# Issuing the loads and stores of the down-projection's weight sums on GpSimd's queue

## The chip, the cores and the metric

The kernel runs on one core of a Trainium2 chip. The metric is the device time of one execution in microseconds. Before the change three runs took 1840.31, 1840.57 and 1843.14 us; the median is 1840.57 us.

The core has five engines with instruction queues of their own: PE (matrix multiply), DVE (vector), ACT (scalar), POOL (GpSimd) and SP (sync). Each works through its queue in order and waits on semaphores for the others. A transfer between DRAM and the on-chip memory is issued by an instruction on one of these queues and then moved by 16 DMA engines, which all queues share. In this kernel nearly all transfers are issued by SP. GpSimd issues a few hundred in the middle of the program, for the attention.

## The reference

The reference is one layer of a diffusion backbone over 1024 latent tokens and 256 context tokens with 1024 channels: modulated norm, one input projection, neighbourhood attention beside a long convolution, an output projection, and then the feed-forward part with which this case is concerned:

```python
h2 = _rmsnorm(x, norm2_g) * (1.0 + sc2) + sh2
u = _dwconv3(h2 @ w_up, ffn_conv_w, ffn_conv_b)
gate, up = jnp.split(u, 2, axis=-1)
x = x + g2 * ((jax.nn.silu(gate) * up) @ w_down)
```

`w_up` is 1024 x 5632 and `w_down` is 2816 x 1024, all in float32. `_dwconv3` is a convolution of width 3 along the tokens.

## The kernel before, in words

A float32 product is made of three matmuls of a split pair (a high part and the rest): `mm3`, lines 116 to 118. `split`, lines 121 and 122, makes the pair: ACT copies the high part (L121), and DVE subtracts it to get the rest (L122).

Both products of the feed-forward part are done with Strassen's scheme in Winograd's form: a product of 2 x 2 blocks takes seven block products in place of eight, at the price of sums of blocks before and after. For the up-projection the sums of the weight blocks are made on DVE as the tiles arrive (L1519 to L1525, tiles `S`). For the down-projection four sums of the blocks of `w_down` are needed, and they are made ahead of time, while the up-projection runs, and kept in a DRAM tensor `tdr`.

The up-projection is a loop over 22 blocks `f` of 128 gate channels and 128 up channels. A step of the loop, in the order of the code, does this:

- load one tile `wt` of the down-projection's weights (L1595): 128 partitions x 2 x 2 x 256 floats, 512 KB, in two transfers of 256 KB, one for each half `r`;
- `up`: load two tiles `wr` of `w_up` (512 KB each, L1503), make the sums, split them into `ws`, and run seven block products on PE, each 24 matmuls, 168 in all. ACT copies some results out (L1547), and DVE adds the others to them into the rows of `rows` (L1552);
- make the four sums in place in `wt` (L1597 to L1600 on DVE, 128 x 256 each), and store the tile to `tdr` (L1602), again in two transfers of 256 KB;
- `conv`: the convolution of the gate rows and of the up rows into `cv` (L1579 on ACT, L1580 and L1581 on DVE), the SiLU (L1604), the product (L1606);
- store the product to `gdr` (L1607, L1608), and, in the first half of the loop, a difference of two halves of it (L1610, L1611) to `sdr` (L1612).

The tile `wt` has one buffer (`bufs=1`). So the next load waits until both stores of the tile before have landed, and the first sum waits until the next load's first half has landed. The tiles `wr` have three buffers.

The order of the instructions on each engine is not that of the code. A scheduler places them by a timeline of its own, so the 22 tiles `wt` do not go one to a step: they are placed as early as the timeline lets them, two to a step, and all 22 are through in the first half of the loop. A change of a queue therefore also moves instructions on the other engines.

The down-projection follows the loop. It reads `gdr`, `sdr` and `tdr` back, and its seven block products use `w_down` itself or the sums. In the changed lines `Q` is SP's queue and `G` is GpSimd's; `wdn` is `w_down` seen by blocks, and `cs` picks a 256 column part of the block.

Of the kernel before, what the change touches and what calls it, by code (L numbers as in the profile page):

```python
# [77 lines left out]
def build(tc, I, O, dbg=None, upto=99):  # L78
    nc = tc.nc
    V, A, G, T, Q = nc.vector, nc.scalar, nc.gpsimd, nc.tensor, nc.sync  # L80
    dbg = dbg or {}
    top = ExitStack()
    with top:
        _build(nc, tc, top, V, A, G, T, Q, I, O, dbg, upto)


def _build(nc, tc, top, V, A, G, T, Q, I, O, dbg, upto):
# [194 lines left out]
    def ft(shape, tag, dt=F32, bufs=1):  # L282
        return fp.tile(shape, dt, tag=tag, name=tag, bufs=bufs)
# [216 lines left out]
    with ies:  # L500
# [3 lines left out]
        for gi, (s, col, tl) in enumerate(groups):  # L504
# [22 lines left out]
            cs = slice(col, col + P * len(tl))  # L527
# [74 lines left out]
    def wsplit(pl, src, scale):  # L602

        i = turn_("w")
        w = pl.tile([P, KC, P], F32, tag=f"wr{i}", name="wr", bufs=1)
        wloads.append(Q.dma_start(out=w, in_=src).ins)
        wh = pl.tile([P, KC, P], F32R, tag=f"wh{i}", name="wh", bufs=1)
        wl = pl.tile([P, KC, P], F32R, tag=f"wl{i}", name="wl", bufs=1)
        if scale == 1.0:
            split(w, wh, wl)  # L610
        else:
            A.activation(wh, w, AF.Copy, scale=scale)
            V.scalar_tensor_tensor(wl, w, scale, wh.bitcast(F32), op0=ALU.mult, op1=ALU.subtract)
        return wh, wl
# [122 lines left out]
    for j in range(4):  # L737
        for which in range(3):
            hy_chunk(which, j)
            if j + which == 0:  # L740

                t = ft([P, 512], "tm", bufs=2)
# [738 lines left out]
    tdr = dr.tile([NI, P, 2, 2, 512], F32, name="tdr")  # L1481
    wdn = I["w_down"][0].rearrange("(r k p) (b c) -> k p r b c", r=2, k=NI, b=2)
    NC = LC + 1 + LL

    def rows():

        t = acp.tile([P, 5 * D], F32, tag="acc", name="rows", bufs=1)
        w = NC + 2
        return [t[:, i * w:(i + 1) * w] for i in range(3)], [t[:, 3 * w + i * NS[1]:3 * w + (i + 1) * NS[1]] for i in range(2)]
# [40 lines left out]
    def up(f, rg, ru):  # L1530

        ws = blocks(f)

        def prod(outs, p, start, stop):
            w = next(ws)
            for s in range(2):
                t = TT[s][p]
                for k in range(4):
                    ks = slice(k * P, (k + 1) * P)
                    mm3(outs[s][:, :NS[s]], w[:, 0, ks], w[:, 1, ks], t[:, 0, k], t[:, 1, k], start and k == 0,  # L1540
                        stop and k == 3)

        def cp(src):
            t = [fpl.tile([P, NS[0]], F32, tag="pc", name="pc", bufs=2), pcb[ring["pc"] % 2]]
            ring["pc"] += 1
            for s in range(2):
                A.copy(t[s], src[s][:, :NS[s]])  # L1547
            return t

        def add(r, cols, x, y):  # L1550
            for s in range(2):
                V.tensor_add(cells(r, cols)[s], j3(x[s]), j3(y[s][:, :NS[s]]))  # L1552

        def two(tag):
            return [bk(tag) for _ in range(2)]

        a = two("a")
        prod(a, 0, True, True)
        p1 = cp(a)
        b = two("b")  # L1560
        prod(b, 1, True, True)
        add(rg, 0, p1, b)
        c = two("c")
        prod(c, 4, True, True)
        p5 = cp(c)
        prod(a, 5, False, True)
        u1 = cp(a)
        prod(c, 2, False, True)
        add(rg, 1, u1, c)
        prod(a, 6, False, True)  # L1570
        add(ru, 1, p5, a)
        d = two("b")
        prod(d, 3, True, True)
        u2 = cp(a)
        add(ru, 0, u2, d)

    def conv(r, ch):
        cv = fpl.tile([P, NC], F32, tag="cv", name="cv", bufs=2)
        A.activation(cv, r[:, 1:NC + 1], AF.Identity, scale=ffw(1, ch), bias=ffb(ch))  # L1579
        V.scalar_tensor_tensor(cv, r[:, 0:NC], ffw(0, ch), cv, op0=ALU.mult, op1=ALU.add)  # L1580
        V.scalar_tensor_tensor(cv, r[:, 2:NC + 2], ffw(2, ch), cv, op0=ALU.mult, op1=ALU.add)  # L1581
        return cv

    for f in range(NFF):
        if f == 0:
            raw, pcb = rows()
            for r in raw:
                for c in (0, LC + 1, NC + 1):
                    G.memset(r[:, c:c + 1], 0.0)
        rg, ru = raw[2 * f % 3], raw[(2 * f + 1) % 3]  # L1590

        i, cs = f // 2, slice(f % 2 * 256, f % 2 * 256 + 256)
        t = fpl.tile([P, 2, 2, 256], F32, tag="wt", name="wt", bufs=1)
        for r in range(2):
            Q.dma_start(out=t[:, r], in_=wdn[i, :, r, :, cs])  # L1595
        up(f, rg, ru)
        V.tensor_sub(t[:, 0, 0], t[:, 0, 1], t[:, 0, 0])  # L1597
        V.tensor_sub(t[:, 0, 1], t[:, 1, 1], t[:, 0, 1])
        V.tensor_sub(t[:, 1, 1], t[:, 1, 1], t[:, 0, 0])
        V.tensor_sub(t[:, 1, 0], t[:, 1, 1], t[:, 1, 0])  # L1600
        for r in range(2):
            Q.dma_start(out=tdr[i, :, r, :, cs], in_=t[:, r])  # L1602
        ga = conv(rg, f)
        A.activation(ga, ga, AF.Silu)  # L1604
        u_ = conv(ru, NFF + f)
        V.tensor_mul(ga, ga, u_)  # L1606
        Q.dma_start(out=gdr[f, :, 0:LC], in_=ga[:, 0:LC])  # L1607
        Q.dma_start(out=gdr[f, :, LC:], in_=ga[:, LC + 1:NC])  # L1608
        if f < NI:
            V.tensor_sub(u_[:, 0:LC], ga[:, 0:LC], ga[:, NR + 1:NR + 1 + LC])  # L1610
            V.tensor_sub(u_[:, LC:NR], ga[:, LC + 1:NR + 1], ga[:, NR + 1 + LC:])  # L1611
            Q.dma_start(out=sdr[f], in_=u_[:, 0:NR])  # L1612
# [20 lines left out]
    def gsplit(src, lasting=None):  # L1633

        if lasting is None:
            hl = dp.tile([P, 2, NR], F32R, tag="gs", name="gs", bufs=3)
            hl = hl[:, 0], hl[:, 1]
        else:
            hl = [dp2.tile([P, NR], F32R, tag=f"X{2 * lasting + x}", name="gx", bufs=1) for x in range(2)]
        split(src, *hl, V)  # L1640
        return hl
# [142 lines left out]
    cs = [(gsplit(Z[i], i - NI + NT), wsplit("4", i, T4)) for i in range(NI - NT, NI)]  # L1784
    for j in range(5):
        for i, (g, w) in enumerate(cs):
            dmm(ps[j], g, w, j, False, i == NT - 1)
        t = dp2.tile([P, 512], F32, tag="fx", name="t", bufs=3)
# [44 lines left out]
```

## Time and profile before

| | |
|---|---|
| median of 3 runs | 1840.57 us |
| the profiled execution, its own time | 1844.13 us |
| its span, first to last instruction | 1841.7 us |
| PE busy | 1719.3 us, 93% of the span |
| DVE busy | 1369.6 us, 74% |
| ACT busy | 893.9 us, 49% |
| GpSimd busy | 396.2 us, 22%; nothing between 1007 and 1700 us |
| DMA queue that SP feeds | 230.75 MB |
| DMA queue that GpSimd feeds | 16.46 MB |
| up-projection's loop | about 995 to 1560 us |
| loads and stores of `wt` issued | 1005.0 to 1278.9 us |

The profile is of one execution, 3.6 us longer than the median of the runs. In the views below the times are microseconds from the start of the span. A row of a timeline has the start, the duration, the engine, the line, the operation with its tiles, and in brackets how long the engine sat idle before it and what released it. Durations of DVE instructions overlap a little with the next one's start (some 0.09 us), so the distance from one start to the next is what counts in a sum. "SPq" and "POOLq" mean the queue of that engine, where an instruction that only issues a transfer is not counted as busy.

### The profile page before, as it was taken

The numbers are of one execution on the slowest core, as the hardware profiler recorded it, in microseconds if no ns is written. First come the engines' busy times: TensorE is split into PE (matmuls) and PEld (weight loads), VectorE is DVE, ScalarE is ACT, GpSimd is POOL, SyncE is SP. The second block draws the span as 40 slices with busy tenths as digits, with TensorE's granted clock in tenths as the row PEclk, the third lists the DMA queues.
The fourth block names the chain that finished last, engine by engine and source line by source line (L and its number), as shares of the span: only waits on it lengthen the run. The fifth ranks groups of instructions, "written<-read, shape, count | busy, mean of one in ns | idle before, by whom it ended". The sixth has DMA issues, their size and how long they took to land.

```text
span 1841.7 us, 27321 instructions
## 1 busy us (share of the span) xinstructions
PE 1719.3 (93%) x9979; PEld 1448.2 (79%) x9979; DVE 1369.6 (74%) x2168; ACT 893.9 (49%) x1852; POOL 396.2 (22%) x487
## 2 busy tenths in 40 slices
PE   5899999999995898898996999999999999999997
PEld 2688788788784455565885999999999999888786
DVE  4668957852778798974568788888777787556797
ACT  4755545532434666665546444444444444443452
POOL 2366655673126432501000000000000000000001
PEclk7999999999996799998998999999999999999999
DMA  7424354356446332516221554454222213934653
GB/s 272 143 75 143 113 169 123 119 146 206 144 140 189 95 113 58 147 47 205 87 97 63 159 173 145 157 163 158 82 68 71 67 57 108 342 113 143 207 185 131
DMA packets 202439, 249.76 MB, mean 136 GB/s; under 512 B 21923, under 2 KB 147988, under 8 KB 202050
## 3 DMA queue, kind: packets, MB, share of 16 engines
q1 hardware_dynamic: 190360, 230.75, 38.9%
q0 software_dynamic: 10240, 16.46, 3.7%
q8 instruction: 78, 1.28, 0.3%
q10 hardware_dynamic: 1705, 0.82, 0.2%
q14 instruction: 56, 0.45, 0.1%
HBM read 176.75 MB, written 71.20 MB: 135 GB/s over the span
## 4 chain that ended last, share of the span: by engine, by line
PE 39%; DVE 14%; DMA 7%; ACT 4%; issue 3%; POOL 2%; SPq 0%; DVEq 0%; POOLq 0%; ACTq 0%
PE psd L118 6%; PE psd L116 6%; PE psd L117 6%; DMA wt<-in_w_down_dram 3%; PE psa L116 2%; PE psa L117 2%; PE psa L118 2%; PE psc L117 2%; PE psc L118 2%; PE psc L116 2%; PE psb L117 2%; PE psb L118 2%; PE psb L116 2%; DMA tdr<-wt 2%; DVE cv L1581 1%
## 5 line engine op out<-in xcount | busy, mean ns | idle before, releaser
L116 PE MATMUL psp<-hh,wh 128*128 128x512 f32 (+1 forms) x552 | 200.7, 364 | 1.9 <-ACT wh L121 1.9
L118 PE MATMUL psp<-hh,wl 128*128 128x512 f32 (+1 forms) x552 | 199.1, 361 | 0.0
L117 PE MATMUL psp<-hl,wh 128*128 128x512 f32 (+1 forms) x552 | 199.1, 361 | 0.0
L1748 POOL TENSOR_TENSOR rs<-rs,mhalf 128x1 f32<-128x1 f32 x10 | 7.7, 775 | 821.6 <-DVE rs L1747 821.6
L116 PE MATMUL psa<-T,ws 128*128 128x256 f32 (+1 forms) x528 | 166.0, 314 | 8.7 <-ACT rows L1547 7.6
L117 PE MATMUL psa<-T,ws 128*128 128x256 f32 (+1 forms) x528 | 165.1, 313 | 0.0
L118 PE MATMUL psa<-T,ws 128*128 128x256 f32 (+1 forms) x528 | 164.6, 312 | 0.0
L116 PE MATMUL psd<-wd,gs 128*128 128x512 f32 x360 | 141.1, 393 | 3.1 <-ACT gs L121 3.1
L117 PE MATMUL psd<-wd,gs 128*128 128x512 f32 x360 | 141.2, 392 | 0.0
L118 PE MATMUL psd<-wd,gs 128*128 128x512 f32 x360 | 125.5, 392 | 1.8 <-DVE gs L122 1.8
L116 PEld LDWEIGHTS psp<-hh,wh 128*128 128x128 f32 x552 | 105.0, 190 | 23.2 <-issue 7.4
L118 PEld LDWEIGHTS psp<-hh,wl 128*128 128x128 f32 x552 | 104.6, 189 | 15.2 <-issue 1.2
L117 PEld LDWEIGHTS psp<-hl,wh 128*128 128x128 f32 x552 | 105.0, 190 | 14.0 <-issue 0.4
L116 PE MATMUL psc<-T,ws 128*128 128x384 f32 (+1 forms) x352 | 110.0, 313 | 6.1 <-ACT ws L121 6.1
L117 PE MATMUL psc<-T,ws 128*128 128x384 f32 (+1 forms) x352 | 110.0, 313 | 0.0
L967 POOL DMA_DIRECT2D tb<-rpw x192 | 100.3, 530 | 45.3 <-DVE m L1089 27.8
L116 PEld LDWEIGHTS psa<-T,ws 128*128 128x128 f32 x528 | 101.3, 192 | 10.7 <-ACT rows L1547 9.0
L118 PE MATMUL psc<-T,ws 128*128 128x384 f32 (+1 forms) x352 | 109.6, 312 | 0.0
L117 PE MATMUL psb<-T,ws 128*128 128x384 f32 (+1 forms) x352 | 109.4, 311 | 0.0
L118 PE MATMUL psb<-T,ws 128*128 128x384 f32 (+1 forms) x352 | 109.4, 311 | 0.0
L116 PE MATMUL psb<-T,ws 128*128 128x384 f32 (+1 forms) x352 | 109.2, 310 | 0.0
L117 PEld LDWEIGHTS psa<-T,ws 128*128 128x128 f32 x528 | 101.2, 192 | 0.0
(404 smaller groups left out, 4771.2 us busy)
## 6 DMA issues: line engine op xcount, KB each, us to landing
wada<-in_w_ada_dram SPq DMA_DIRECT2D x48, 512.0 KB
wr<-in_w_up_dram SPq DMA_DIRECT2D x44, 512.0 KB
gr<-gdr SPq DMA_DIRECT2D x44, 320.0 KB
wr<-in_w_in_dram SPq DMA_DIRECT2D x23, 512.0 KB
wt<-in_w_down_dram SPq DMA_DIRECT2D x44, 256.0 KB
tdr<-wt SPq DMA_DIRECT2D x44, 256.0 KB
gdr<-cv SPq DMA_DIRECT2D x22, 512.0 KB
wr<-tdr SPq DMA_DIRECT2D x20, 512.0 KB
```

The lines of the kernel that those rows point to most:

```text
L116: T.matmul(out, ah, bh, start=start, stop=False, skip_group_check=True)
L117: T.matmul(out, ah, bl, start=False, stop=False, skip_group_check=True)
L118: T.matmul(out, al, bh, start=False, stop=stop, skip_group_check=True)
L967: blast[0] = G.dma_start(out=tv[:, :, a * 8:a * 8 + 64], in_=rpw[var, :, 2 * p_:2 * p_ + 2, :, d * 8:d * 8 + 64].rearrange("q h u x -> q ( ...
L1581: V.scalar_tensor_tensor(cv, r[:, 2:NC + 2], ffw(2, ch), cv, op0=ALU.mult, op1=ALU.add)
L1748: G.tensor_tensor(rs, rs, mhalf, op=ALU.pow)
```

## The change

The two loads of a tile `wt` and the two stores of its sums are issued on GpSimd's queue in place of SP's. What is transferred, the tile and its one buffer, and the arithmetic are the same.

```diff
         t = fpl.tile([P, 2, 2, 256], F32, tag="wt", name="wt", bufs=1)
         for r in range(2):
-            Q.dma_start(out=t[:, r], in_=wdn[i, :, r, :, cs])
+            G.dma_start(out=t[:, r], in_=wdn[i, :, r, :, cs])
         up(f, rg, ru)
         V.tensor_sub(t[:, 0, 0], t[:, 0, 1], t[:, 0, 0])
         V.tensor_sub(t[:, 0, 1], t[:, 1, 1], t[:, 0, 1])
         V.tensor_sub(t[:, 1, 1], t[:, 1, 1], t[:, 0, 0])
         V.tensor_sub(t[:, 1, 0], t[:, 1, 1], t[:, 1, 0])
         for r in range(2):
-            Q.dma_start(out=tdr[i, :, r, :, cs], in_=t[:, r])
+            G.dma_start(out=tdr[i, :, r, :, cs], in_=t[:, r])
```

The scheduler places the instructions anew. Three places matter; each repeats in every step while there are tiles `wt` to be made.

**Gap A, on DVE**, in a step of the loop: the rows from the last sum of one tile `wt` (L1600) to the first sum of the next (L1597). Before:

```order
L1600 TENSOR_TENSOR wt<-wt 128x256
L1521 TENSOR_TENSOR S<-S,wr 128x512
L122 TENSOR_TENSOR ws<-wr,ws 128x512
L1552 TENSOR_TENSOR rows<-pc,psc 128x256
L1552 TENSOR_TENSOR rows<-rows,psc 128x3x128
L122 TENSOR_TENSOR ws<-wr,ws 128x512
L1552 TENSOR_TENSOR rows<-pc,psa 128x256
L1597 TENSOR_TENSOR wt<-wt 128x256
```

In the changed kernel, the same place:

```order
L1600 TENSOR_TENSOR wt<-wt 128x256
L122 TENSOR_TENSOR ws<-wr,ws 128x512
L1552 TENSOR_TENSOR rows<-pc,psc 128x256
L1552 TENSOR_TENSOR rows<-rows,psc 128x3x128
L122 TENSOR_TENSOR ws<-wr,ws 128x512
L1552 TENSOR_TENSOR rows<-pc,psa 128x256
L1580 SCALAR_TENSOR_TENSOR cv<-rows,vec,cv 128x1281
L1597 TENSOR_TENSOR wt<-wt 128x256
```

L1521 has left the gap (it now stands ahead of L1600), and the convolution's L1580 has come into it.

**Gap B, on DVE**, the other one of the same step. Before:

```order
L1600 TENSOR_TENSOR wt<-wt 128x256
L122 TENSOR_TENSOR ws<-S,ws 128x512
L1523 TENSOR_TENSOR S<-wr,S 128x512
L1580 SCALAR_TENSOR_TENSOR cv<-rows,vec,cv 128x1281
L122 TENSOR_TENSOR ws<-S,ws 128x512
L1581 SCALAR_TENSOR_TENSOR cv<-rows,vec,cv 128x1281
L1552 TENSOR_TENSOR rows<-pc,psb 128x256
L1525 TENSOR_TENSOR S<-wr 128x512
L1597 TENSOR_TENSOR wt<-wt 128x256
```

In the changed kernel:

```order
L1600 TENSOR_TENSOR wt<-wt 128x256
L1523 TENSOR_TENSOR S<-wr,S 128x512
L1580 SCALAR_TENSOR_TENSOR cv<-rows,vec,cv 128x1281
L122 TENSOR_TENSOR ws<-S,ws 128x512
L1552 TENSOR_TENSOR rows<-pc,psb 128x256
L1581 SCALAR_TENSOR_TENSOR cv<-rows,vec,cv 128x1281
L1525 TENSOR_TENSOR S<-wr 128x512
L1552 TENSOR_TENSOR rows<-rows,psb 128x3x128
L1606 TENSOR_TENSOR cv<-cv 128x1281
L122 TENSOR_TENSOR ws<-S,ws 128x512
L1597 TENSOR_TENSOR wt<-wt 128x256
```

One L122 has left it, and an L1552, the product L1606 and another L122 have come in.

**The queues.** On SP a step of the loop before (`wr` is a tile of `w_up`, `gdr` and `sdr` take the results):

```order
L1602 DMA tdr<-wt 128x2x256
L1612 DMA sdr<-cv 128x640
L1602 DMA tdr<-wt 128x2x256
L1503 DMA wr<-in_w_up_dram 128x8x128
L1595 DMA wt<-in_w_down_dram 128x2x256 x2
L1602 DMA tdr<-wt 128x2x256 x2
L1595 DMA wt<-in_w_down_dram 128x2x256 x2
L1503 DMA wr<-in_w_up_dram 128x8x128
L1607 DMA gdr<-cv 128x256
L1608 DMA gdr<-cv 128x1024
```

In the changed kernel a step on SP:

```order
L1503 DMA wr<-in_w_up_dram 128x8x128 x2
L1607 DMA gdr<-cv 128x256
L1608 DMA gdr<-cv 128x1024
L1612 DMA sdr<-cv 128x640
L1503 DMA wr<-in_w_up_dram 128x8x128 x2
```

and on GpSimd, from the last work ahead of the loop:

```order
L1287 TENSOR_TENSOR rs<-rs,mhalf 128x1 x20
L1595 DMA wt<-in_w_down_dram 128x2x256 x2
L1589 MEMSET rows 128x1 x9
L1602 DMA tdr<-wt 128x2x256 x2
L1595 DMA wt<-in_w_down_dram 128x2x256 x2
L1602 DMA tdr<-wt 128x2x256 x2
```

The loads and stores of `wt` have left SP and follow each other on GpSimd, whose queue holds nothing else from there to the end of the loop but the nine L1589 rows.

## The prediction

> **What bounds the kernel now.** I looked first at the stretches of the up-projection's loop, one with tiles `wt` in work and one after the last of them (columns: busy time of PE, weight loads, DVE, ACT, GpSimd, with counts; granted clock; share of the DMA engines; GB/s).
>
> ```profile
> 1100.00:1200.00 100.00, 97.73 (x660) 97.33 (x659) 86.82 (x134) 44.46 (x72) 0.00 (x0) 1.00 0.50 160
> 1400.00:1500.00 100.00, 100.00 (x677) 100.00 (x676) 77.68 (x97) 45.24 (x72) 0.00 (x0) 1.00 0.23 69
> ```
>
> PE is the bound after the tiles are done: no idle time, 677 matmuls in 100 us. While they are in work it does 660. DVE is busy for 86.8 us of 100, so busy time alone does not make it the bound. Next I read the waits of the loop.
>
> ```profile
> DVE wt L1597 <- DMA wt<-in_w_down_dram: 36.0, 12, 5.0
> ACT rows L1547 <- DVE rows L1552: 52.9, 22, 5.9
> ...
> PE psa L116 <- ACT rows L1547: 7.6, 7, 2.1
> ```
>
> DVE waits 36.0 us for loads of `wt`, 12 times, and this is handed on: ACT waits for DVE, PE for ACT. Third, the row of that wait in successive steps of the loop.
>
> ```profile
> 1028.73 0.43 DVE L1597 TENSOR_TENSOR wt<-wt 128x256 f32<-128x256 f32 x1 [4.20 <-DMA wt<-in_w_down_dram]
> ...
> 1054.62 0.42 DVE L1597 TENSOR_TENSOR wt<-wt 128x256 f32<-128x256 f32 x1 [3.65 <-DMA wt<-in_w_down_dram]
> ...
> 1080.44 0.42 DVE L1597 TENSOR_TENSOR wt<-wt 128x256 f32<-128x256 f32 x1 [3.59 <-DMA wt<-in_w_down_dram]
> ...
> 1106.42 0.43 DVE L1597 TENSOR_TENSOR wt<-wt 128x256 f32<-128x256 f32 x1 [3.75 <-DMA wt<-in_w_down_dram]
> ...
> 1132.99 0.42 DVE L1597 TENSOR_TENSOR wt<-wt 128x256 f32<-128x256 f32 x1 [4.31 <-DMA wt<-in_w_down_dram]
> ...
> 1157.59 0.42 DVE L1597 TENSOR_TENSOR wt<-wt 128x256 f32<-128x256 f32 x1 [2.38 <-DMA wt<-in_w_down_dram]
> ```
>
> The steps are 25.89, 25.82, 25.98, 26.57 and 24.60 us long. Less the wait at their end they are 22.24, 22.23, 22.23, 22.26 and 22.22. So in this stretch DVE, its wait included, sets the pace: **step = 22.24 us + wait**. What PE needs shows in the same DVE row before and after the tiles run out.
>
> ```profile
> 1023.92 0.61 DVE L1552 TENSOR_TENSOR rows<-pc,psa 128x256 f32<-128x256 f32 x1
> ...
> 1281.93 0.63 DVE L1552 TENSOR_TENSOR rows<-pc,psa 128x256 f32<-128x256 f32 x1
> ...
> 1306.80 0.62 DVE L1552 TENSOR_TENSOR rows<-pc,psa 128x256 f32<-128x256 f32 x1
> ```
>
> From 1281.93 to 1306.80 is a step bound by PE: 24.87 us. From 1023.92 to 1281.93 are ten steps, 258.0 us, where PE would need 248.7. All that can be won in steady state is **9.3 us**; a wait of up to 24.87 - 22.24 = 2.63 us in a step costs nothing.
>
> **The change part by part.** One turnaround of the tile in gap A before (the queue of SP, then DVE, then ACT):
>
> ```profile
> 1226.23 0.37 SPq L1602 DMA_DIRECT2D tdr<-wt  x1
> 1227.44 0.38 SPq L1503 DMA_DIRECT2D wr<-in_w_up_dram  x1
> 1228.44 1.21 SPq L1595 DMA_DIRECT2D wt<-in_w_down_dram  x2
> ...
> 1226.13 0.68 DVE L1521 TENSOR_TENSOR S<-S,wr 128x512 f32<-128x512 f32 x1
> 1226.73 0.68 DVE L122 TENSOR_TENSOR ws<-wr,ws 128x512 fp32r<-128x512 f32 x1
> ...
> 1233.11 0.43 DVE L1597 TENSOR_TENSOR wt<-wt 128x256 f32<-128x256 f32 x1 [3.15 <-DMA wt<-in_w_down_dram]
> 1233.45 1.55 DVE L1580 SCALAR_TENSOR_TENSOR cv<-rows,vec,cv 128x1281 f32<-128x1281 f32 x1
> 1234.91 0.42 DVE L1598 TENSOR_TENSOR wt<-wt 128x256 f32<-128x256 f32 x1
> ...
> 1228.81 1.47 ACT L1579 ACTIVATE cv<-rows,vec 128x1281 f32<-128x1281 f32 x1 [0.29 <-DVE rows L1552]
> ```
>
> L1600 ends at 1226.13; the store goes out 0.10 us later and takes 2.21 us until the next load may go; the load takes 4.67 us until L1597 runs. Turnaround T = 6.98 us. The load stood on SP's queue behind a 512 KB tile of `w_up` issued 1.00 us ahead of it.
>
> *Issue time.* 44 loads and 44 stores leave SP. In a step that takes 2 x 1.21 us of load issues and 4 x 0.37 us of stores off its queue. SP has no arithmetic, and what is queued behind these issues, the tiles of `w_up`, does not hold DVE up here (the step less its wait for `wt` is the same 22.24 each time), so I count this as nothing. If that cover were gone, a tile of `w_up` would land earlier, which is a gain. GpSimd has nothing else to do but nine L1589 rows, which now stand behind the first two issues; what they clear is read first by the convolution at the end of the first step. The 88 issues on GpSimd delay nobody else.
>
> *The gaps.* What counts is T on the new queue against the DVE work that stands in the gaps in the new order. Gap A: from L122 (1226.73) to the point where L1597 was ready, 1233.11 - 3.15 = 1229.96, are 3.23 us. L1580 joins; its input from ACT is there at 1228.81 + 1.47 = 1230.28, 0.32 us later, and it takes 1233.45 to 1234.91 = 1.46 us. Gap A is then 3.23 + 0.32 + 1.46 = 5.0 us, **5.1** with a hand-over. Gap B is, in the new order, the run that before went from L1523 to L1598, without the L1597 in it:
>
> ```profile
> 1214.97 0.69 DVE L1523 TENSOR_TENSOR S<-wr,S 128x512 f32<-128x512 f32 x1
> ...
> 1220.09 0.42 DVE L1597 TENSOR_TENSOR wt<-wt 128x256 f32<-128x256 f32 x1
> 1220.42 0.86 DVE L1552 TENSOR_TENSOR rows<-rows,psb 128x384 f32<-128x384 f32 x1
> ...
> 1223.11 0.42 DVE L1598 TENSOR_TENSOR wt<-wt 128x256 f32<-128x256 f32 x1
> ```
>
> 1223.11 - 1214.97 - 0.33 = **7.8** us. So the wait in a step is now max(0, T - 5.1) + max(0, T - 7.8).
>
> *T on GpSimd's queue.* No GpSimd transfer of this size and kind is in the trace. The nearest (KB each and median us from issue to landing, then the spreads):
>
> ```profile
> tb<-rpw POOLq DMA_DIRECT2D x192, 32.0 KB, 2.6
> q<-qd POOLq DMA_DIRECT2D x4, 640.0 KB, 4.8
> rpw<-rp POOLq DMA_DIRECT2D x3, 240.0 KB, 4.5
> ...
> L558 POOL DMA_DIRECT2D rpw<-rp x3: 604/607/632, 390.6 to 445.8; - x3
> DMA to landing us min/median/max: 3.9/4.5/4.6
> ...
> L980 POOL DMA_DIRECT2D q<-qd x4: 567/568/594, 538.9 to 743.7; - x4
> DMA to landing us min/median/max: 4.2/4.8/6.0
> ...
> L967 POOL DMA_DIRECT2D tb<-rpw x192: 528/528/556, 545.3 to 771.0; - x192
> DMA to landing us min/median/max: 2.0/2.6/8.3
> ```
>
> Store: `rpw` (L558) is 240 KB into DRAM, median 4.5, least 3.9. Load: between 32 KB (2.6) and 640 KB (4.8), 256 KB comes to 2.6 + 2.2 x 224/608 = 3.4; from the least of each, 2.0 + 2.2 x 224/608 = 2.8. With 0.1 for hand-over the medians give T = 8.0, the least ones 6.8. Two of the three `rpw` stores went out while the DMA engines were nearly full:
>
> ```profile
> 390.60:395.20 4.60, 4.60 (x31) 4.12 (x30) 0.16 (x1) 1.11 (x4) 0.64 (x2) 1.00 0.91 286
> 445.80:449.80 4.00, 4.00 (x22) 3.36 (x21) 0.00 (x0) 0.96 (x2) 0.60 (x1) 1.00 0.96 356
> ```
>
> Share 0.91 and 0.96, against 0.50 in the loop. The load also no longer stands in line behind the `w_up` tile. So I take the middle of the two, **T = 7.4**. Both ends: a store as fast as SP's (2.2) and the least load give 5.1; the slowest store (4.6) and the slowest `q` load (6.0) give 10.7.
>
> *The sum.* T = 7.4: wait 2.3 + 0, DVE would need 24.54 us a step, less than PE's 24.87. Ten steps take 248.7 in place of 258.0: 9.3 us less. The start of the loop is left out: the first load waits there for the same DVE work as before, and the first sums come a little later in DVE's order, which is worth under 1 us either way. The down-projection's few moved rows carry the same work and count as nothing; if they had no cover, that is one DVE row, 0.7 us. The profiled execution, 1844.13 us with 1841.7 us of span, would become 1834.8. It lies 3.56 us above the median of the runs, so against the median the forecast is 1840.57 - 9.3 = **1831.3 us**.
>
> The page "DMA: Bandwidth & Descriptors" of the Trainium skill (§ Issuing engines are not separate DMA queues) speaks against the change: transfers issued by different engines run on the same 16 DMA engines, and issuing from several saves only issue time. By that rule the sum is the issue time, nothing here. The same page (§ Anatomy of one DMA, SWDGE path) fits a GpSimd transfer as 2.0 us + bytes/436e3; that estimate is 2.6 us for 256 KB, T = 5.3 and the sum 9.3. The `rpw` rows, 3.9 to 4.6 us for 240 KB, do not agree with it.
>
> **The rivals.** *GpSimd's turnaround is longer than both gaps.* From T = 7.8 gap B waits as well and each us of T costs 2 us a step. The tie with the 25.80 us mean step of before comes at 22.24 + (T - 5.1) + (T - 7.8) = 25.80, T = 8.23. For it: the median rows give 8.0 already, and single ones are longer. Against: the loop's DMA share is half. At T = 8.8 the wait is 3.7 + 1.0 = 4.7, the step 26.94, ten steps 269.4, 11.4 us more: **1852**.
>
> *It comes out even.* The stall only changes its cause: T from 8.04 to 8.42 gives steps of 25.42 to 26.18 us and a change within 3.7 us, **1840.6** at 8.23. This is also where an issue-time-only change would land.
>
> *DVE starves GpSimd.* If GpSimd could only write a transfer's descriptors between DVE instructions, each transfer in the chain could wait out one L1580 (1.46 us): T = 7.4 + 2.9 = 10.3, wait 5.2 + 2.5, step 29.9, ten steps 41 us more: **1882**. Against it: the 192 `tb` issues (L967) take 528 to 556 ns without exception, in a stretch where DVE is busy:
>
> ```profile
> 600.00:700.00 100.00, 90.06 (x507) 52.46 (x509) 89.77 (x196) 62.52 (x203) 48.19 (x91) 0.89 0.40 104
> ```
>
> The page "SBUF — State Buffer" of the Trainium skill (§ 🔬 SBUF: two separate sides) describes such a lock for DVE instructions in a 2-port mode and says in § Who interferes with whom that `tensor_tensor` has none; the L967 row agrees that issues are not held up.
>
> *The new order on DVE is what helps, whatever the queue.* Then T may be as before (6.98) and the wait is 1.9: PE bound, the same 1831. It differs from the forecast only in what to credit.
>
> **How the numbers follow.** What a measurement of this kernel can tell from no change is about 0.2%, 3.7 us. Faster by more needs T under 8.04: 0.55, nearly all of it the forecast (T 6.8 to 7.9 gives 9.3). Even: 0.15. Slower by more, T over 8.42: 0.30, of which 0.04 is the starved case. The low end: a PE step as short as 24.60 (the last one above) and 0.9 at the start give 12.9 less, 1828; the high end is T = 8.75, 1851. The tail of T to 10.7 (step 30.7, some 1890) is left out, at about 1 in 8. Alone the forecast's own range is 1828 to 1837.
>
> **What would show it.** Right: the row L1597 waits under 2.6 us a step, nearly all in gap A; the step 24.6 to 24.9 us; the PE wait of L116 for L1547 near zero; stores of `tdr` on GpSimd land in about 4.2 us and loads in about 3.1. Wrong: L1597 waits twice a step, the 36.0 us grows, steps beyond 25.8; or DVE and `tdr` as forecast, but the step is set by something that I took for cover.

## The result, and the profile after

The changed kernel took 1853.6 us (median of 4 runs, 1851.6 to 1856.2), the kernel before 1841.8 us in the same comparison (median of 4, 1840.3 to 1843.1). The ratio is 1.0059, 95% interval 1.0041 to 1.0078: about 11 us slower (11.8 by the two medians). The forecast was 1831.3 us. No ratio below counts the two of the twelve runs of the kernel with the stores alone moved that took 3353 us; what held those up is open. The profiled execution of the changed kernel took 1856.21 us, its span is 1854.4 us.

The first view is the stretch of the loop with tiles `wt` in work, and one after the last of them (columns as in the prediction).

```profile
1100.00:1200.00 100.00, 91.92 (x607) 91.10 (x606) 78.23 (x122) 39.53 (x63) 21.12 (x29) 0.99 0.44 149
1400.00:1500.00 100.00, 100.00 (x677) 100.00 (x676) 78.17 (x98) 45.58 (x73) 0.00 (x0) 1.00 0.23 69
```

After the tiles are done nothing differs: 677 matmuls in 100 us, as before. While they are in work PE does 607 of them, where it did 660. The row of DVE that marked the steps in the prediction says how much that is.

```profile
1027.19 0.62 DVE L1552 TENSOR_TENSOR rows<-pc,psa 128x256 f32<-128x256 f32 x1
...
1297.05 0.63 DVE L1552 TENSOR_TENSOR rows<-pc,psa 128x256 f32<-128x256 f32 x1
```

These are again ten steps: 269.86 us, 258.01 before. The difference is 11.85 us, nearly all of the 12.7 us by which the two spans differ. (The loop began 2.7 us later in this profile and took 0.6 us longer up to the first marker; what follows the ten steps took 2.4 us less.) The waits of the loop (us in total, times, longest):

```profile
ACT rows L1547 <- DVE rows L1552: 56.7, 22, 6.7
...
DVE wt L1597 <- DMA wt<-in_w_down_dram: 31.9, 11, 4.7
...
DVE S L1519 <- DMA wr<-in_w_up_dram: 28.9, 20, 3.4
...
PE psa L116 <- ACT rows L1547: 14.8, 8, 3.4
```

The wait for `wt` has gone down by only 4 us (36.0 before), and a second one has grown: L1519 waits for the tile `wr` of `w_up`. Before, its row was:

```profile
DVE S L1519 <- DMA wr<-in_w_up_dram: 16.3, 11, 3.6
```

Both totals are over the whole loop. In the ten steps L1519 waits 11.4 us now and did not wait at all before; the rest fell outside them, at the start and in the second half of the loop. Now one step, on DVE:

```profile
1205.63 0.68 DVE L1525 TENSOR_TENSOR S<-wr 128x512 f32<-128x512 f32 x1
...
1208.92 0.42 DVE L1597 TENSOR_TENSOR wt<-wt 128x256 f32<-128x256 f32 x1
...
1211.73 0.69 DVE L1519 TENSOR_TENSOR S<-wr 128x512 f32<-128x512 f32 x1 [1.59 <-DMA wr<-in_w_up_dram]
...
1214.21 0.42 DVE L1600 TENSOR_TENSOR wt<-wt 128x256 f32<-128x256 f32 x1
...
1218.02 1.56 DVE L1580 SCALAR_TENSOR_TENSOR cv<-rows,vec,cv 128x1281 f32<-128x1281 f32 x1 [0.48 <-ACT cv L1579]
1222.52 0.43 DVE L1597 TENSOR_TENSOR wt<-wt 128x256 f32<-128x256 f32 x1 [2.95 <-DMA wt<-in_w_down_dram]
```

Gap B (ending at 1208.92) does not wait, gap A (1214.55 to 1222.52) waits 2.95 us after 5.0 us. Between the two DVE now stands 1.59 us at L1519, and 0.48 of the 5.0 us in gap A are a wait of L1580 for ACT. The queues of the same step (GpSimd, then SP):

```profile
1201.55 0.74 POOL L1602 DMA_DIRECT2D tdr<-wt  x1 [1.55 <-DVE wt L1600]
1204.71 1.45 POOL L1595 DMA_DIRECT2D wt<-in_w_down_dram  x2 [2.42 <-DMA tdr<-wt]
1213.06 0.73 POOL L1602 DMA_DIRECT2D tdr<-wt  x1 [6.90 <-DVE wt L1598]
1214.93 0.73 POOL L1602 DMA_DIRECT2D tdr<-wt  x1 [1.15 <-DVE wt L1600]
1219.40 1.45 POOL L1595 DMA_DIRECT2D wt<-in_w_down_dram  x2 [3.74 <-DMA tdr<-wt]
...
1206.38 0.38 SPq L1503 DMA_DIRECT2D wr<-in_w_up_dram  x1
...
1215.26 0.38 SPq L1503 DMA_DIRECT2D wr<-in_w_up_dram  x1
```

The turnaround of gap A is T = 1222.52 - 1214.55 = 7.97 us: 0.38 from the end of L1600 to the store, 4.47 from the store to the load, 3.12 from the load to L1597. In gap B the same store needs 3.16 (1201.55 to 1204.71). What differs is the tile of `w_up`: in gap A it goes out on SP's queue 0.33 us behind the store. Over the whole loop:

```profile
DMA to landing us min/median/max: 2.9/3.2/5.1
...
DMA to landing us min/median/max: 2.5/2.6/5.6
```

The first row is of the loads (L1595), the second of the stores (L1602). What moved in gap A, first in the changed kernel, then in the kernel before (the last two columns are the share of the DMA engines and GB/s; the stretches run from the store's issue to the load's issue and on to L1597):

```profile
1214.90:1217.00 2.10, 2.10 (x18) 2.10 (x17) 2.10 (x5) 1.10 (x2) 0.73 (x1) 1.00 0.20 57
1217.00:1219.40 2.40, 2.40 (x17) 2.40 (x16) 1.92 (x3) 1.72 (x3) 0.00 (x0) 1.00 0.93 306
1219.40:1220.50 1.10, 1.10 (x10) 1.10 (x9) 0.17 (x1) 0.15 (x1) 1.10 (x2) 1.00 0.00 0
1220.50:1222.50 2.00, 2.00 (x13) 2.00 (x13) 0.00 (x0) 0.00 (x0) 0.35 (x1) 1.00 0.72 234
```

```profile
1226.23:1228.44 2.21, 2.21 (x17) 2.21 (x16) 2.21 (x4) 0.55 (x1) 0.00 (x0) 1.00 0.65 236
1228.44:1229.96 1.52, 1.52 (x13) 1.52 (x12) 1.48 (x3) 1.23 (x2) 0.00 (x0) 1.00 0.86 238
1229.96:1233.11 3.15, 3.15 (x24) 3.15 (x23) 0.00 (x1) 1.18 (x3) 0.00 (x0) 1.00 0.68 217
```

In the kernel before the DMA engines are at work from the store's issue on. With GpSimd's queue they move little in the first 2.1 us, and nothing of this store: what moves first, up to 1215.30, is the rest of the other half's store. Split by queue (q0 is GpSimd's, q1 is SP's; packets, MB, share), first 1215.30 to 1217.00, then 1217.00 to 1218.40:

```profile
q1 hardware_dynamic: 104, 0.05, 13.1%
tdr<-wt POOLq DMA_DIRECT2D x1, 256.0 KB, 3.9
...
q1 hardware_dynamic: 439, 0.22, 55.2%
q0 software_dynamic: 79, 0.26, 46.0%
```

The 256 KB of the store (0.26 MB) begin 2.1 us after the issue and move together with 0.22 MB of the `w_up` tile; they land 3.9 us after the issue (second row). In gap B the store begins 1.3 us after its issue and lands after 2.6. In the first 1.1 us in which GpSimd then issues the two loads nothing moves at all.

### The profile page after: what moved, and what is told of

Same layout as the page of the kernel before. It is cut to its first block, busy times and chain, and to the rows that moved or that the text cites. A ratio compares the mean times of both kernels' runs of the same rounds, so it can differ in the third digit from the quotient of the medians.

```text
span 1854.4 us, 27356 instructions
## 1 busy us (share of the span) xinstructions
PE 1722.3 (93%) x9979; PEld 1451.6 (78%) x9979; DVE 1365.8 (74%) x2168; ACT 892.2 (48%) x1852; POOL 461.9 (25%) x575
## 5 line engine op out<-in xcount | busy, mean ns | idle before, releaser
L116 PE MATMUL psd<-wd,gs 128*128 128x512 f32 x360 | 140.0, 390 | 3.5 <-ACT gs L121 3.5
L117 PE MATMUL psd<-wd,gs 128*128 128x512 f32 x360 | 140.1, 389 | 0.0
L118 PE MATMUL psd<-wd,gs 128*128 128x512 f32 x360 | 123.6, 390 | 2.4 <-DVE gs L122 2.4
```

The costliest lines, as they stand in the source:

```text
L116: T.matmul(out, ah, bh, start=start, stop=False, skip_group_check=True)
L117: T.matmul(out, ah, bl, start=False, stop=False, skip_group_check=True)
L118: T.matmul(out, al, bh, start=False, stop=stop, skip_group_check=True)
```

## The experiments

Three theories went into them. *Queue*: a transfer that GpSimd issues takes longer, and that is all. *Shared engines*: with two queues the transfers of `wt` and the `w_up` tiles move at the same time, and each makes the other late. *Order*: the new order of DVE's rows causes the new wait at L1519. DVE's rows ahead of the loop stand in the same order in these kernels, but that stretch varied by up to 9 us from profile to profile (it was longest in the profile of the kernel with the stores alone moved, and one row stood elsewhere in one of them), so each kernel is judged by its ten steps as well as by its time. Each ratio is against the kernel before.

**Only the loads moved.**

```diff
-            Q.dma_start(out=t[:, r], in_=wdn[i, :, r, :, cs])
+            G.dma_start(out=t[:, r], in_=wdn[i, :, r, :, cs])
```

> Only the loads of wt on GpSimd's queue, the stores of tdr back on SP's. Three theories. Queue: a transfer issued by GpSimd takes longer (store 4.4 us where SP's took 2.2), and that alone lengthens the turnaround of wt. Shared engines: wt's transfers and the w_up tiles (wr), now on two queues, are in flight together and make each other late; that gives the 4.4 us store in gap A (3.15 in gap B, where no wr is under way) and the new wait of L1519 for wr. Order: the new order of DVE's rows asks for wr (L1519) earlier after its buffer comes free (L1525), so L1519 waits whatever the queues do. Queue: store 2.2 + load 3.1 + hand-over, T about 5.5, wait at L1597 0.4 us in gap A, none at L1519, bound by PE: 1831. Shared engines: the load in gap A goes out beside wr, 3.1 + 1.3 = 4.4, T 6.8, wait 1.7; in gap B the load is done before wr is issued, so no wait at L1519; still under PE's step: 1831 to 1835. Order: DVE's order in gap A is that of the change, in gap B that of before, so nothing at L1519 either: 1831. All three say faster; what tells them apart is the wait in gap A.

Ratio 0.9992 (0.9979 to 1.0006), ten steps 251.1 us. Run again:

> The kernel with only the loads on GpSimd's queue once more, since its ten steps were 6.9 us shorter than before and its median only 1.9 us. If the loop's gain is real, the ten steps are again 250 to 252.5 us and the two sets of runs together are 0.1 to 0.35% faster than before. If it was one lucky profile, the ten steps are 255 or more.

Ratio 0.9977 (0.9963 to 0.9991), ten steps 248.9 us, which is PE's own time. The gain in the loop came again, 7 and 9 us; in total it comes out as 0.1 and 0.2%, the first not clear of noise. T in gap A is 6.1 to 8.0 us in the second profile. All three theories had said faster; the wait for `wt`, nearly all in gap A, is 1.9 us a step (2.4 in the first profile), nearer the 1.7 of shared engines than the 0.4 of the queue theory, though in some steps the gap stood in the old order, with 3.6 us of work in place of 5.0, which adds to it. The parts of T are not those of shared engines, though: in 13 of the 18 gaps A of the two profiles the load took 2.9 to 3.6 us, near the 3.1 of the queue theory, and it was the store, still on SP's queue, that needed 2.7 to 3.8 where it had mostly needed 2.2 before. That the sum came near is luck.

**Only the stores moved.**

```diff
-            Q.dma_start(out=tdr[i, :, r, :, cs], in_=t[:, r])
+            G.dma_start(out=tdr[i, :, r, :, cs], in_=t[:, r])
```

> Only the stores on GpSimd's queue, the loads of wt back on SP's, ahead of or behind the w_up tiles in one line. DVE's order is that of the change but for one row each way in gap B. Queue: the slow store stays (4.4), T about 7.5 to 8, wait at L1597 about 2.5 to 3 us, nothing at L1519: step 25.2 to 25.7, total 1835 to 1840. Shared engines: the store in gap A still runs beside wr (4.4), but the load of wt in gap B is on the same queue as wr and ahead of it, so L1519 waits under 0.3 us: step about 25.5, total 1836 to 1841. Order: L1519 still waits 1 us or more in each step: step 26.5 to 27, total 1847 to 1853.

Ratio 1.0015 (1.0003 to 1.0027), ten steps 257.2 us. DVE's order is nearly that of the change, and the 12 us are gone, so the order alone does not cost them. Most of the difference to the change is the wait for `wt`, 24.0 us in place of 33.0. What is left of its part shows too: L1519 waits 0.8 us a step (0.3 had been expected by shared engines, 1 or more by order), L1580 0.5. The store in gap A, beside the `w_up` tile again (SP, then GpSimd):

```profile
1211.35 0.38 SPq L1503 DMA_DIRECT2D wr<-in_w_up_dram  x1
1214.98 1.21 SPq L1595 DMA_DIRECT2D wt<-in_w_down_dram  x2
...
1211.02 0.72 POOL L1602 DMA_DIRECT2D tdr<-wt  x1 [2.47 <-DVE wt L1600]
```

From store to load 3.96 us, and 4.47 with the load on GpSimd: both stores landed after 3.9 us, and SP takes up the landing half a microsecond sooner.

**Both on ScalarE's queue.**

```diff
-            Q.dma_start(out=t[:, r], in_=wdn[i, :, r, :, cs])
+            A.dma_start(out=t[:, r], in_=wdn[i, :, r, :, cs])
...
-            Q.dma_start(out=tdr[i, :, r, :, cs], in_=t[:, r])
+            A.dma_start(out=tdr[i, :, r, :, cs], in_=t[:, r])
```

> Loads and stores both on ScalarE's queue, whose descriptors no program on GpSimd writes: again apart from the w_up tiles. Queue: store 2.2, load 2.7, T about 6 with up to 1 us lost behind an activation, wait at L1597 about 1 us, no wait at L1519: bound by PE, 1831. Shared engines: store and load in gap A are each longer beside wr, T about 7.5, and L1519 waits for wr 1 us or more in each step: step 25.3 to 26.3, total 1836 to 1846. Order: as shared engines for L1519, since the order of DVE's rows is near that of the change, but a turnaround of 6.

Ratio 0.9979 (0.9965 to 0.9993), ten steps 250.3 us. Gap A (a tile of `w_up` 0.60 us behind the store), then gap B without one, on ACT's queue, and between them the row of DVE that waits:

```profile
1081.96 0.37 ACTq L1602 DMA_DIRECT2D tdr<-wt  x1
1084.72 0.55 ACTq L1595 DMA_DIRECT2D wt<-in_w_down_dram  x1
...
1086.89 1.55 DVE L1580 SCALAR_TENSOR_TENSOR cv<-rows,vec,cv 128x1281 f32<-128x1281 f32 x1 [2.06 <-ACT cv L1579]
1088.36 0.42 DVE L1597 TENSOR_TENSOR wt<-wt 128x256 f32<-128x256 f32 x1
...
1094.17 0.37 ACTq L1602 DMA_DIRECT2D tdr<-wt  x1
1096.41 1.22 ACTq L1595 DMA_DIRECT2D wt<-in_w_down_dram  x2
```

The store needs 2.76 us beside the tile and 2.24 alone: a second queue costs 0.5 here, 1.3 on GpSimd. So neither theory alone is right. The turnaround is 6.2 to 6.6 us in most gaps A, but the wait has only moved: ACT now stands for the landing of the store, and DVE for ACT (18.2 us at L1580 in ten steps, 2.6 at L1597).

**The change with half of each `w_up` tile.**

```diff
-        Q.dma_start(out=w if len(src.shape) == 2 else w.rearrange("p (k c) -> p k c", k=KC), in_=src)
+        k = KC // 2; Q.dma_start(out=w.rearrange("p (k c) -> p k c", k=KC)[:, :k], in_=src[:, :k])
...
-        a11, a12, a21, a22 = wg[:, 0:512], wg[:, 512:], wu[:, 0:512], wu[:, 512:]
+        a11, a12, a21, a22 = wg[:, 0:512], wg[:, 0:512], wu[:, 0:512], wu[:, 0:512]
```

> The change with half of every w_up tile left out: only the first 4 of 8 blocks are loaded (256 KB in place of 512) and the sums on DVE read that half twice, so the work on DVE, ACT and PE and the order of all engines are those of the change; the up-projection's values are not the reference's. Queue: the store in gap A stays at 4.4 us and L1597 waits 3.0 us a step; L1519 no longer waits since a half tile lands early: step 25.5, total 1838 to 1841. Shared engines: the store in gap A falls from 4.4 toward the 3.15 of gap B, under 4.0, and the wait at L1597 to 2.5 or less; no wait at L1519; step 24.9 to 25.2, total 1831 to 1835. Order: L1519's wait goes, the wait at L1597 stays, as by the queue theory.

Ratio 0.9960 (0.9943 to 0.9977), ten steps 248.5 us, all bound by PE. DVE's order is that of the change but for a few rows in the first two steps. Gap A in a late step (GpSimd, then SP):

```profile
1242.27 0.73 POOL L1602 DMA_DIRECT2D tdr<-wt  x1 [1.14 <-DVE wt L1600]
1245.45 1.45 POOL L1595 DMA_DIRECT2D wt<-in_w_down_dram  x2 [2.45 <-DMA tdr<-wt]
...
1243.37 0.38 SPq L1503 DMA_DIRECT2D wr<-in_w_up_dram  x1
```

From store to load 3.18 us, and 3.42 in a step where the tile went out 0.57 us behind the store. The 4.47 us of the change are therefore not what a GpSimd store takes in that place: 1.0 to 1.3 us of it come from the `w_up` tile beside it. The queue theory said 4.4 here, and falls. The tile is not only shorter in this run: in most steps it also goes out later, 1.1 to 1.4 us behind the store where it was 0.33. In the one step of the ten where it goes out 0.32 us behind, the store took 4.03 us, so by this one step the distance counts at least as much as the size.

**Its control, on SP's queue.** The same two edits in the kernel before.

> The control of the run with half w_up tiles: the kernel before (everything on SP's queue) with only the first half of every w_up tile loaded and read twice; the up-projection's values are not the reference's. With GpSimd's queue that took the store in gap A from 4.4 to 3.3 us and the ten steps from 269.9 to 248.5. On SP's queue the store goes ahead of the w_up tile in one line, so by shared engines it should stay near 2.2 us; the load, which stands behind that tile, should shorten by about the time of 256 KB, from 4.67 to 3.6 or so, T to 6: the wait of 3.6 us a step falls to about 2.5 and the ten steps from 258.0 to about 249; total 1831 to 1834. If half tiles help by something else than the transfers' overlap (DVE, ACT or PE faster), the second half of the loop would show it too, below 24.87 us a step.

Ratio 1.0024 (1.0008 to 1.0040), ten steps 258.2 us: the expectation failed. T did fall, to some 6.4 us in gap A from 7.2. But the scheduler placed L1597 earlier in both gaps (3.0 to 3.6 us of work in most gaps A where there were 3.6 to 4.2, 4.9 in every other gap B where there were 5.8), and DVE waits 33.5 us for `wt`, as before. Since the order moved, this run is no clean control of the one above; it shows that a shorter turnaround which the placement spends again wins nothing. Half tiles do not speed up anything else: the second half of the loop stays at 24.87 us a step in both kernels.

**All three kinds on GpSimd's queue.** The change, with the `w_up` tiles moved there too.

```diff
-        Q.dma_start(out=w if len(src.shape) == 2 else w.rearrange("p (k c) -> p k c", k=KC), in_=src)
+        G.dma_start(out=w if len(src.shape) == 2 else w.rearrange("p (k c) -> p k c", k=KC), in_=src)
```

> The change, with the w_up tiles (wr) moved to GpSimd's queue too: one line again for the three kinds of transfer, the store of gap A issued ahead of the w_up tile. Shared engines: the store is no longer overlapped by the tile and falls from 4.4 to the 3.1 to 3.2 us that it takes alone; the load stands behind the tile, 3.1 to 4.2; T 6.9 to 7.7, the wait at L1597 2 to 2.6 a step; the tile itself, a GpSimd transfer now, lands 1 us later or more, so L1519 waits 1 to 2 us: step 26 to 27, total 1843 to 1856. Queue: the 4.4 us is what a GpSimd store takes in that place whatever is beside it, with a load of 3.7 or more behind the tile: T over 8.5, step 28 and more, total 1860 or more.

Ratio 1.0057 (1.0037 to 1.0078), ten steps 265.1 us. Gap A on GpSimd's queue:

```profile
1242.59 0.73 POOL L1602 DMA_DIRECT2D tdr<-wt  x1 [4.58 <-DVE wt L1600]
1243.31 0.90 POOL L1503 DMA_DIRECT2D wr<-in_w_up_dram  x1
1245.71 1.43 POOL L1595 DMA_DIRECT2D wt<-in_w_down_dram  x2 [1.49 <-DMA tdr<-wt]
```

In one line with the full tile behind it, 0.72 us now, the store is back at 3.12 us, as shared engines said (3.1 in most steps of the loop); how much of this is the one line and how much the longer distance this run does not tell. What was won at L1597 (2.2 us a step, 3.2 with the change) is lost at L1519: the `w_up` tile lands in 5.2 us now (median), and L1519 waits 1.7 us a step.

**One tile to a step.** In both kernels ScalarE copies one column of the step before into the tile ahead of its load; the load overwrites it. The rows of DVE then stand in the same order on either queue.

```diff
-        t = fpl.tile([P, 2, 2, 256], F32, tag="wt", name="wt", bufs=1)
+        t = fpl.tile([P, 2, 2, 256], F32, tag="wt", name="wt", bufs=1); f and A.copy(t[:, 0, 0, 0:1], raw[2 * (f - 1) % 3][:, 1:2])
```

> The change, with one tile of wt in each of the 22 steps instead of two in each of the first eleven: before its load, ScalarE copies one column of the step before into the tile, so the load cannot go ahead of that. The turnaround then has most of a step of 24.87 us for itself. If the slowdown is the turnaround of one buffer against short gaps (whether from GpSimd's queue or from shared engines), L1597 waits for nothing, every step is PE's 24.87, the ten steps that took 269.9 us take 249, and the total is 1831 to 1834. If GpSimd's transfers cost DVE or the w_up tiles time in themselves, whatever the slack (L1519 waiting more than 2.6 us a step, slower DVE rows), steps stay above 25 us, now in both halves of the loop: 1840 or more. If the down-projection is held up because the last sums are stored only at the end of the loop, the loop is as fast but the end comes 3 to 5 us later: 1835 to 1838.

> The kernel before with the same spreading, everything on SP's queue. The rows of DVE stand in the same order as in the other spread kernel, so the two differ in the queue alone. If only slack matters both are alike, 1831 to 1834, within 0.2% of each other. If a separate queue makes the w_up tiles late (shared engines), L1519 waits less here than with GpSimd's queue, by about 1 us a step, under PE's cover in both. If the old load behind a w_up tile on one queue matters, L1597 waits here and not there.

On GpSimd's queue 0.9959 (0.9941 to 0.9977), ten steps 249.9 us; on SP's 0.9961 (0.9946 to 0.9976), ten steps 248.3. Both beat both kernels, by about 7 us against before, and with the same order of rows and room for the turnaround the queue makes no difference that is clear of noise. L1597 still waited for loads on GpSimd's queue, 9.9 us in five of the ten steps, where nothing had been expected. One expectation was wrong in sign: L1519 waits longer with SP's queue (23.6 us in ten steps) than with GpSimd's (12.0), under PE's cover in both.

Put together, the waits of DVE in the ten steps add up to the steps: 22.24 us, from the prediction, plus a tenth of the waits (us, summed over the rows of DVE's timeline between the two marker rows). This is bookkeeping: it shows that DVE's own rows take the same time in all six kernels and that no wait is missing, not where the waits come from.

| kernel | for `wt` | L1519 for `wr` | L1580 for ACT | 22.24 + sum/10 | step measured |
|---|---|---|---|---|---|
| before | 35.0 | 0 | 0 | 25.74 | 25.80 |
| the change | 33.0 | 11.4 | 4.4 | 27.12 | 26.99 |
| loads alone (first) | 23.8 | 2.7 | 2.3 | 25.12 | 25.11 |
| stores alone | 24.0 | 8.0 | 4.9 | 25.93 | 25.72 |
| ScalarE's queue | 2.6 | 9.4 | 18.2 | 25.26 | 25.03 |
| all on GpSimd | 22.3 | 17.0 | 4.2 | 26.59 | 26.51 |

Where the sum stays under PE's 24.87 (loads alone again, half tiles with the change) the step is PE's.

## Why the prediction was wrong, point by point

*The bound and the formula* held in part. With DVE's wait for `wt` alone, as the prediction had it, the formula gives the change 22.24 + 3.3 = 25.5 us a step, and 26.99 were measured. With the waits at L1519 and L1580 added it gives every step of the table to within 0.25 us, and where the waits stay under PE's cover the ten steps take the 248.7 us that the prediction worked out (248.3 to 249.9 in four runs).

*The gaps* held: 5.1 and 7.8 us were forecast, 5.0 and 7.75 were measured. But the prediction used 0.32 us of gap A twice: while L1580 waits for ACT DVE does no work, so this covers some of T and lengthens the step as well. With the 0.32, T = 7.4 gives 24.86 and not 24.54; measured it was 0.44 us a step.

*T on GpSimd's queue* was mis-sized: 7.4 us taken, 7.9 to 8.2 measured in gap A, once 9.7. Its load was right (3.4 by the medians, 3.0 to 3.3 measured), its store was right by the median `rpw` row (4.5 against 4.4 to 4.7, once 6.1), and the hand-over was 0.38 and not 0.1. The match of the store is partly luck: the `rpw` row is a landing, the store of gap A landed after 3.9 us, and the rest is the time until GpSimd issued the load. (Over the loop the stores landed in 2.6 us, and not in the 4.2 that the prediction named as a sign of being right.) What failed is the choice to take the middle between the median rows and the least ones because "the loop's DMA share is half". Half is a mean over 100 us. In the 2.4 us in which the store's second half moves the share is 0.93, as high as it was beside two of the `rpw` rows, because the `w_up` tile stands right behind it. With T = 8.0 the formula gives a wait of 2.9 + 0.2 and a step of 25.3 us; with the 0.44 at L1580 it is 25.8, the step of before. So these two errors cost the whole gain that was forecast, but they do not make the kernel slower.

*"Issue time ... counted as nothing"* is the step that turned the sign: the wait at L1519, 1.14 us a step and 11.4 us in ten. The prediction named the cover (L1519 finds its tile there) and looked only at one way in which it could go, a tile that lands earlier. It lands later. Before (SP's queue, then DVE):

```profile
1216.56 1.21 SPq L1595 DMA_DIRECT2D wt<-in_w_down_dram  x2
1220.24 0.38 SPq L1503 DMA_DIRECT2D wr<-in_w_up_dram  x1
...
1219.48 0.68 DVE L1525 TENSOR_TENSOR S<-wr 128x512 f32<-128x512 f32 x1
1224.25 0.68 DVE L1519 TENSOR_TENSOR S<-wr 128x512 f32<-128x512 f32 x1
```

The load of `wt` goes out 3.7 us ahead of the `w_up` tile of gap B, and L1519, 4.2 us after that tile's buffer came free, never waits. With the change the load goes out later, after a longer store, 1.7 us ahead (1204.71 and 1206.38); the tile lands 5.3 us after its buffer came free (median of the steps that wait), and DVE's new order asks for it after 3.9. So the order asks 0.3 us sooner, and the rest is the tile. What moves from the tile's issue to the first packet of the `gdr` stores that follow it on SP's queue, before (1220.24 to 1223.46), then with the change (1206.38 to 1209.40):

```profile
q1 hardware_dynamic: 1043, 0.53, 57.5%
...
q0 software_dynamic: 148, 0.48, 44.7%
q1 hardware_dynamic: 672, 0.34, 38.3%
```

Before, the whole tile (0.52 MB) has moved in that stretch. With the change 0.34 MB of it have, since 0.48 MB of the load of `wt` move beside it, and the rest then moves together with the 640 KB of the `gdr` stores. Call the time from the load's issue to the tile's the lead. With the stores alone moved it is 2.2 us in most steps and the tile lands after about 4.9; on ScalarE's queue 2.9 and 4.2. The four kernels line up, but no run changed this lead alone, so that the lead is the cause is argued and not shown. A late tile does not even need a second queue: with one tile `wt` to a step, all on SP's queue, half of the load goes out 1.75 us ahead, the `gdr` stores follow it just ahead of the tile, and the tile lands about 7 us after its buffer came free. That the wait is not DVE's order alone is shown by the run with half tiles, which has nearly that order and 0.2 us of this wait in ten steps.

*The rivals.* "GpSimd's turnaround is longer than both gaps" came nearest in time (1852), but that is luck, since its mechanism is not what happened: gap B waited in a single step of the ten, and the second us a step came from L1519. "DVE starves GpSimd" falls: the 88 issues take 727 to 764 ns. "The new order on DVE is what helps" is not borne out: the run with the stores alone has nearly that order and gains 0.8 us in ten steps. Two steps of the ten, 28.7 us long, had a store or load of 5 to 6 us in them; what held those up is open.

*The pages.* The Trainium skill, "DMA: Bandwidth & Descriptors", § Anatomy of one DMA, gave an estimate of 2.6 us for 256 KB; the stores landed in 2.6 (median of 44), so it holds where nothing is beside them (the loads landed in 3.2, the store of gap A in 3.9). The prediction was wrong to set it aside as the price of a store, but the T of 5.3 us made from it would have been further off: the next load went out 3.1 us after a store with nothing beside it, 4.4 in gap A. The same page, § Queues, rings and completion order, says that each DMA engine takes turns between the queues that have work; the trace agrees, with 0.26 MB of GpSimd's store and 0.22 MB of SP's tile in the same 1.4 us.

## What to carry to other kernels

A second queue does not only take issue time off the first: it gives up the order in which one line moves its transfers, so look at what is issued within a microsecond or two of each transfer that somebody waits for, and read the DMA share of those stretches, not the mean. When a cover is named ("the tile is there in time"), write down by how much it is in time and what will shift on both ends. Where one buffer's turnaround stalls an engine, spreading its uses over more of the work did at least as well here (0.4%) as the best choice of queue (0.1 to 0.2%; the intervals overlap).

## What the runs showed of the hardware

- A 256 KB store issued by GpSimd and alone lands after 2.6 us and lets the next load on its queue go after 3.1; on SP's and ScalarE's queues the load goes after 2.1 to 2.3.
- With a 512 KB transfer on SP's queue 0.3 us behind it, GpSimd's store needs 4.4 to 4.7 us until the next load (once 6.1); ScalarE's needs 2.5 to 2.8 with such a transfer 0.6 us behind it.
- From the end of DVE's L1600 to the issue of the store that waits for it GpSimd takes 0.38 us, SP and ScalarE 0.10.
- While GpSimd issued two 256 KB loads (1.45 us) the DMA engines stood empty for the first 1.1 us.
